# Laplacian filter: two adjacent image rows per partition instead of two half images, without pad columns

One core of a Trainium2 chip runs the kernel. The metric is the device time of one execution in microseconds, lower is better. The kernel before takes 40.27 us (median of 15 runs, 40.21 to 40.34).

## The reference

Input and output are float32 arrays of shape 8 x 3 x 256 x 256, that is 24 images of 256 KB each. Every image gets a five-point Laplacian whose missing neighbours at the border are the border pixels themselves.

```python
def reference(x):
    output = np.zeros_like(x)
    for b in range(batch):
        for ch in range(c):
            output[b, ch] = ndimage.laplace(x[b, ch])   # up + down + left + right - 4 * centre
    return output
```

6.29 MB are read and 6.29 MB are written. Nothing can be left out of either.

## The kernel before

Four images form a group of 1 MB; there are six groups. Partition `pp` holds row `pp` (half `h2 = 0`) and row `pp + 128` (half `h2 = 1`) of each image. The two rows are far apart in DRAM, so each contiguous run is one row: 1 KB. The tile has a pad column on either side of each row.

```python
raw = sbuf.tile([P, GROUP, 2, WP], fp32, name="raw", tag="raw")       # WP = W + 2
src = xi[g * GROUP:(g + 1) * GROUP].rearrange("img (h2 pp) w -> pp img h2 w", h2=2)
nc.sync.dma_start(out=raw[:, :, :, 1:W + 1], in_=src)                 # all six loads first
# ... then for each group:
nc.gpsimd.tensor_copy(out=raw[:, :, :, 0:1], in_=raw[:, :, :, 1:2])   # pads, on POOL
nc.gpsimd.tensor_copy(out=raw[:, :, :, WP - 1:WP], in_=raw[:, :, :, W:W + 1])
# ... three matmuls per 128x512 chunk (vertical terms, the other half's edge row, left neighbour)
nc.scalar.copy(out=oa, in_=pas[pr])                                   # PSUM to SBUF
nc.vector.tensor_add(out=oa, in0=oa, in1=r0)                          # right neighbour, float32
# ...
nc.scalar.dma_start(out=dst, in_=ot)                                  # store, issued by ACT
```

The matmuls read the upper two bytes of each float32 as bf16. Their weights (diagonals and single points) are built on POOL.

Of the kernel before, what the change touches and what calls it, by code (L numbers as in the profile page):

```python
# [1 line left out]

# [4 lines left out]


def _set_point(nc, mat_ap, p, f, val, n=128):  # L10
    cm = n + 1
    base = -(p * cm - f)
    nc.gpsimd.affine_select(  # L13
        out=mat_ap,
        in_=mat_ap,
        compare_op=mybir.AluOpType.not_equal,
        fill=float(val),
        base=base,
        pattern=[[-1, n]],
        channel_multiplier=cm,  # L20
    )


def _set_diagonal(nc, mat_ap, off, val, n=128):
    nc.gpsimd.affine_select(  # L25
        out=mat_ap,
        in_=mat_ap,
        compare_op=mybir.AluOpType.not_equal,
        fill=float(val),
        base=off,  # L30
        pattern=[[-1, n]],
        channel_multiplier=1,
    )


@with_exitstack
def kernel(
    ctx: ExitStack,
    tc: tile.TileContext,
    x: bass.AP,  # L40
    out: bass.AP,
):
    nc = tc.nc
    P = 128

    fp32 = mybir.dt.float32
    bf16 = mybir.dt.bfloat16

    B, C, H, W = x.shape
    assert H == 256 and W == 256  # L50
    NIMG = B * C
    xi = x.rearrange("b c h w -> (b c) h w")
    oi = out.rearrange("b c h w -> (b c) h w")

    GROUP = 4
    NG = NIMG // GROUP
    NPAIR = GROUP // 2
    WP = W + 2

    const_pool = ctx.enter_context(tc.tile_pool(name="consts", bufs=1))  # L60

    A = const_pool.tile([P, P], bf16, name="A_mat")
    Cm = const_pool.tile([P, P], bf16, name="C_mat")
    BT = const_pool.tile([P, P], bf16, name="BT_mat")
    Bm = const_pool.tile([P, P], bf16, name="B_mat")
    Ident = const_pool.tile([P, P], bf16, name="I_mat")

    nc.gpsimd.memset(A, 0.0)
    _set_diagonal(nc, A, 1, 1.0)
    _set_diagonal(nc, A, -1, 1.0)  # L70
    _set_diagonal(nc, A, 0, -4.0)
    _set_point(nc, A, 0, 0, -3.0)

    nc.gpsimd.memset(Cm, 0.0)
    _set_diagonal(nc, Cm, 1, 1.0)
    _set_diagonal(nc, Cm, -1, 1.0)
    _set_diagonal(nc, Cm, 0, -4.0)
    _set_point(nc, Cm, 127, 127, -3.0)

    nc.gpsimd.memset(BT, 0.0)  # L80
    _set_point(nc, BT, 0, 127, 1.0)

    nc.gpsimd.memset(Bm, 0.0)
    _set_point(nc, Bm, 127, 0, 1.0)

    nc.gpsimd.memset(Ident, 0.0)
    _set_diagonal(nc, Ident, 0, 1.0)

    sbuf = ctx.enter_context(tc.tile_pool(name="sbuf", bufs=6))
    psum = ctx.enter_context(tc.tile_pool(name="psum", bufs=4, space=bass.MemoryType.PSUM))  # L90

    raws = []
    for g in range(NG):
        raw = sbuf.tile([P, GROUP, 2, WP], fp32, name="raw", tag="raw")
        src = xi[g * GROUP:(g + 1) * GROUP].rearrange(
            "img (h2 pp) w -> pp img h2 w", h2=2
        )
        nc.sync.dma_start(out=raw[:, :, :, 1:W + 1], in_=src)
        raws.append(raw)

    for g in range(NG):
        raw = raws[g]
        nc.gpsimd.tensor_copy(out=raw[:, :, :, 0:1], in_=raw[:, :, :, 1:2])  # L103
        nc.gpsimd.tensor_copy(out=raw[:, :, :, WP - 1:WP], in_=raw[:, :, :, W:W + 1])  # L104

        rb = raw.bitcast(bf16)
        rb = rb.rearrange("pp img h (c two) -> pp img h c two", two=2)
        rb = rb[:, :, :, :, 1]

        ot = sbuf.tile([P, GROUP, 2, W], fp32, name="ot", tag="ot")  # L110

        pas = []
        pbs = []
        for pr in range(NPAIR):
            pas.append(psum.tile([P, 2, W], fp32, name="pa", tag="pa"))
            pbs.append(psum.tile([P, 2, W], fp32, name="pb", tag="pb"))

        def t0b(pr):
            i0 = 2 * pr
            return rb[:, i0:i0 + 2, 0, 1:W + 1]  # L120

        def t1b(pr):
            i0 = 2 * pr
            return rb[:, i0:i0 + 2, 1, 1:W + 1]

        def lshift_b(pr, h):
            i0 = 2 * pr
            return rb[:, i0:i0 + 2, h, 0:W]

        for pr in range(NPAIR):  # L130
            nc.tensor.matmul(pas[pr], A, t0b(pr), start=True, stop=False)  # L131
        for pr in range(NPAIR):
            nc.tensor.matmul(pbs[pr], Cm, t1b(pr), start=True, stop=False)  # L133
        for pr in range(NPAIR):
            nc.tensor.matmul(pas[pr], BT, t1b(pr), start=False, stop=False)  # L135
        for pr in range(NPAIR):
            nc.tensor.matmul(pbs[pr], Bm, t0b(pr), start=False, stop=False)  # L137
        for pr in range(NPAIR):
            nc.tensor.matmul(pas[pr], Ident, lshift_b(pr, 0), start=False, stop=True)  # L139
            nc.tensor.matmul(pbs[pr], Ident, lshift_b(pr, 1), start=False, stop=True)  # L140

        for pr in range(NPAIR):
            i0 = 2 * pr
            oa = ot[:, i0:i0 + 2, 0, :]
            ob = ot[:, i0:i0 + 2, 1, :]
            r0 = raw[:, i0:i0 + 2, 0, 2:WP]
            r1 = raw[:, i0:i0 + 2, 1, 2:WP]
            nc.scalar.copy(out=oa, in_=pas[pr])  # L148
            nc.vector.tensor_add(out=oa, in0=oa, in1=r0)  # L149
            nc.scalar.copy(out=ob, in_=pbs[pr])  # L150
            nc.vector.tensor_add(out=ob, in0=ob, in1=r1)  # L151

        dst = oi[g * GROUP:(g + 1) * GROUP].rearrange(
            "img (h2 pp) w -> pp img h2 w", h2=2
        )
        nc.scalar.dma_start(out=dst, in_=ot)  # L156


# [1 line left out]
_INS = ['x']  # L160
_OUTS = [((8, 3, 256, 256), 'float32')]


# [23 lines left out]
```

## Time and profile before

| | before |
|---|---|
| time, median | 40.27 us |
| span in the profile | 38.5 us |
| bytes moved, mean rate over the span | 12.58 MB, 327 GB/s |
| last store issued | 28.7 us |

The page of the profiled run, in this order: busy time of each engine; the busy share of the 16 DMA engines in 40 slices of the span; what they moved in each slice; the packet count; the shares of the chain of waits that ended last; and two groups of instructions (busy us and mean ns, then idle time before them).

```profile
PE 19.3 (50%) x72; PEld 7.3 (19%) x72; DVE 15.0 (39%) x24; ACT 13.7 (36%) x25; POOL 8.1 (21%) x32
...
DMA  0059989999999999999999999999999999999910
GB/s 0 6 176 381 387 275 318 379 362 352 347 349 347 351 348 349 348 346 349 356 387 387 387 383 386 388 383 387 388 383 387 387 386 386 386 385 387 334 46 0
DMA packets 12480, 12.58 MB, mean 327 GB/s; under 512 B 192, under 2 KB 12480, under 8 KB 12480
...
PE 23%; DMA 15%; ACT 11%; DVE 10%; issue 8%; POOL 2%; DVEq 2%; ACTq 1%; POOLq 0%
...
L103 POOL COPY raw<-raw 128x8 f32<-128x8 f32 x6 | 2.1, 358 | 15.3 <-DMA raw<-in_x_dram 15.3
...
L104 POOL COPY raw<-raw 128x8 f32<-128x8 f32 x6 | 2.6, 433 | 0.0
```

No compute engine is busy for much more than half of the span (PE 50%). The DMA row is at nine tenths almost throughout. All packets are under 2 KB; in the trace's single records, 12,288 of them are 1,024 bytes and 192 are the 4-byte completion marks. What the profile calls a packet is one contiguous run. The Trainium skill, "DMA: Bandwidth & Descriptors", section "Why a DMA increments its semaphore by 16 and not by 1", says that one descriptor moves one contiguous run, so the profile's packets are the skill's descriptors. The chain of waits names compute engines.

The view by stretches of time shows, per line, a stretch of the span, the busy time of each engine in it, the granted clock, the DMA share and, last, GB/s.

```profile
core 0: us, PE busy (x) PEld busy (x) DVE busy (x) ACT busy (x) POOL busy (x), PEclk, DMA share, GB/s
8.00:14.50 6.50, 6.43 (x21) 2.17 (x20) 2.50 (x4) 2.49 (x5) 1.46 (x5) 1.00 1.09 349
14.50:18.30 3.80, 3.80 (x18) 1.62 (x17) 3.31 (x6) 3.11 (x8) 1.18 (x2) 1.00 1.09 348
19.30:28.00 8.70, 6.56 (x28) 2.42 (x26) 7.49 (x13) 6.05 (x12) 0.85 (x3) 1.00 1.09 386
```

There are two rates: 348 to 349 GB/s while there are only loads, and 386 GB/s once stores run. In the single records a 1 KB packet takes 51 ns in the first case and 46 ns in the second.

The timeline of ACT shows the first and the last store being issued (start, duration, what).

```profile
14.53 0.41 ACTq L156 DMA_DIRECT2D out_dram<-ot  x1
...
28.72 0.69 ACTq L156 DMA_DIRECT2D out_dram<-ot  x1
```

The last store is issued at 28.72 us and the span ends at 38.5 us.

### The profile page before, as it was taken

To read this page: it belongs to the slowest core of one execution; us is meant where nothing else is said; L and a number is where in the kernel's file an instruction comes from. 1 tells how busy PE (TensorE), PEld (TensorE's weight loads), DVE (VectorE), ACT (ScalarE), POOL (GpSimd) and SP (SyncE) were. 2 spreads that over 40 slices of the span, in tenths; PEclk is the share of its full clock that TensorE was granted. 3 is DMA by queue.
4 is the path that set the end of the run, shared out by engine and by line. 5 is a ranking of instruction groups with operands and counts; after the bars stand their busy time and mean duration, and the time that the engine had idled before them with its cause. 6 is when DMAs were issued, how large, how long until landed. Compare 5 with 4: busy or idle time off the path is not lost.

```text
span 38.5 us, 302 instructions
## 1 busy us (share of the span) xinstructions
PE 19.3 (50%) x72; PEld 7.3 (19%) x72; DVE 15.0 (39%) x24; ACT 13.7 (36%) x25; POOL 8.1 (21%) x32
## 2 busy tenths in 40 slices
PE   0000002999999999999999989991000000000000
PEld 0001001332133444344434414330000000000000
DVE  0000000000019946998999996399870000000000
ACT  2900000000089339759795950993900000000000
POOL 4999102001400900830710007000000000000000
PEclk9999999999999999999999999999995555555555
DMA  0059989999999999999999999999999999999910
GB/s 0 6 176 381 387 275 318 379 362 352 347 349 347 351 348 349 348 346 349 356 387 387 387 383 386 388 383 387 388 383 387 387 386 386 386 385 387 334 46 0
DMA packets 12480, 12.58 MB, mean 327 GB/s; under 512 B 192, under 2 KB 12480, under 8 KB 12480
## 3 DMA queue, kind: packets, MB, share of 16 engines
q1 hardware_dynamic: 6240, 6.29, 49.8%
q10 hardware_dynamic: 6240, 6.29, 46.0%
HBM read 6.29 MB, written 6.29 MB: 327 GB/s over the span
## 4 chain that ended last, share of the span: by engine, by line
PE 23%; DMA 15%; ACT 11%; DVE 10%; issue 8%; POOL 2%; DVEq 2%; ACTq 1%; POOLq 0%
DMA raw<-in_x_dram 15%; ACT ot L148 9%; DVE ot L149 7%; PE pa L139 6%; PE pb L140 4%; DVE ot L151 4%; PE pa L135 4%; PE pa L131 4%; PE pb L133 3%; PE pb L137 3%; ACT ot L150 2%; DVEq L182 2%; ACTq L156 1%; POOL raw L103 1%; POOL raw L104 1%
## 5 line engine op out<-in xcount | busy, mean ns | idle before, releaser
L149 DVE TENSOR_TENSOR ot<-ot,raw 128x512 f32<-128x512 f32 x12 | 8.3, 688 | 13.7 <-ACT ot L148 12.6
L148 ACT COPY ot<-pa 128x512 f32<-128x512 f32 x12 | 7.1, 594 | 13.4 <-PE pa L139 10.9
L151 DVE TENSOR_TENSOR ot<-ot,raw 128x512 f32<-128x512 f32 x12 | 8.2, 682 | 0.0
L131 PE MATMUL pa<-raw,A_mat 128*128 128x512 bf16 x12 | 4.4, 427 | 6.7 <-DMA raw<-in_x_dram 6.7
L150 ACT COPY ot<-pb 128x512 f32<-128x512 f32 x12 | 7.2, 602 | 0.0
L103 POOL COPY raw<-raw 128x8 f32<-128x8 f32 x6 | 2.1, 358 | 15.3 <-DMA raw<-in_x_dram 15.3
L139 PE MATMUL pa<-raw,I_mat 128*128 128x512 bf16 x12 | 5.1, 426 | 0.1
L140 PE MATMUL pb<-raw,I_mat 128*128 128x512 bf16 x12 | 5.1, 425 | 0.0
L133 PE MATMUL pb<-raw,C_mat 128*128 128x512 bf16 x12 | 4.6, 431 | 0.0
L137 PE MATMUL pb<-raw,B_mat 128*128 128x512 bf16 x12 | 4.6, 429 | 0.0
L135 PE MATMUL pa<-raw,BT_mat 128*128 128x512 bf16 x12 | 4.5, 430 | 0.0
L131 PEld LDWEIGHTS <-A_mat 128*128 128x128 bf16 x12 | 1.2, 101 | 8.6 <-issue 4.0
L104 POOL COPY raw<-raw 128x8 f32<-128x8 f32 x6 | 2.6, 433 | 0.0
L139 PEld LDWEIGHTS <-I_mat 128*128 128x128 bf16 x12 | 1.2, 101 | 2.6 <-POOL I_mat L25 1.0
L135 PEld LDWEIGHTS <-BT_mat 128*128 128x128 bf16 x12 | 1.3, 105 | 1.9 <-issue 0.6
L137 PEld LDWEIGHTS <-B_mat 128*128 128x128 bf16 x12 | 1.3, 105 | 1.9 <-issue 0.6
L133 PEld LDWEIGHTS <-C_mat 128*128 128x128 bf16 x12 | 1.3, 105 | 1.8 <-issue 0.3
L148 ACT ACT_TABLE_LOAD x1 | 1.3, 1283 | 0.7 <-PEq L171 0.7
L140 PEld LDWEIGHTS <-I_mat 128*128 128x128 bf16 x12 | 1.2, 102 | 1.6 <-issue 0.3
L25 POOL TENSOR_SCALAR_AFFINE_SELECT A_mat<-A_mat 128x128 bf16<-128x128 bf16 x3 | 0.9, 296 | 0.0
L25 POOL TENSOR_SCALAR_AFFINE_SELECT C_mat<-C_mat 128x128 bf16<-128x128 bf16 x3 | 0.9, 296 | 0.0
L13 POOL TENSOR_SCALAR_AFFINE_SELECT BT_mat<-BT_mat 128x128 bf16<-128x128 bf16 x1 | 0.3, 298 | 0.0
(13 smaller groups left out, 2.6 us busy)
## 6 DMA issues: line engine op xcount, KB each, us to landing
raw<-in_x_dram SPq DMA_DIRECT2D x6, 1024.0 KB, 11.2
out_dram<-ot ACTq DMA_DIRECT2D x6, 1024.0 KB, 9.3
```

What stands on the lines that cost most here:

```text
L103: nc.gpsimd.tensor_copy(out=raw[:, :, :, 0:1], in_=raw[:, :, :, 1:2])
L104: nc.gpsimd.tensor_copy(out=raw[:, :, :, WP - 1:WP], in_=raw[:, :, :, W:W + 1])
L131: nc.tensor.matmul(pas[pr], A, t0b(pr), start=True, stop=False)
L133: nc.tensor.matmul(pbs[pr], Cm, t1b(pr), start=True, stop=False)
L135: nc.tensor.matmul(pas[pr], BT, t1b(pr), start=False, stop=False)
L137: nc.tensor.matmul(pbs[pr], Bm, t0b(pr), start=False, stop=False)
L139: nc.tensor.matmul(pas[pr], Ident, lshift_b(pr, 0), start=False, stop=True)
L140: nc.tensor.matmul(pbs[pr], Ident, lshift_b(pr, 1), start=False, stop=True)
L148: nc.scalar.copy(out=oa, in_=pas[pr])
L149: nc.vector.tensor_add(out=oa, in0=oa, in1=r0)
L150: nc.scalar.copy(out=ob, in_=pbs[pr])
L151: nc.vector.tensor_add(out=ob, in0=ob, in1=r1)
```

## The change

Each partition takes two *adjacent* rows, `2p` and `2p + 1`. Each run then is 2 KB on both sides. Because there are no pad columns, the border's left and right terms are added by POOL to the finished output, two columns at once. The matrices change with the rows: `U` and `L` each add the row above and the row below in one matmul, so the count of 72 matmuls stays.

```diff
-        raw = sbuf.tile([P, GROUP, 2, WP], fp32, name="raw", tag="raw")
+        raw = sbuf.tile([P, GROUP, 2, W], fp32, name="raw", tag="raw")
-            "img (h2 pp) w -> pp img h2 w", h2=2
+            "img (pp two) w -> pp img two w", two=2        # for the load and for the store
-        nc.sync.dma_start(out=raw[:, :, :, 1:W + 1], in_=src)
+        nc.sync.dma_start(out=raw, in_=src)
-        nc.gpsimd.tensor_copy(out=raw[:, :, :, 0:1], in_=raw[:, :, :, 1:2])
-        nc.gpsimd.tensor_copy(out=raw[:, :, :, WP - 1:WP], in_=raw[:, :, :, W:W + 1])
 ...
+                nc.tensor.matmul(pts[pr][s][:, :, 1:W], Ident, sub(pr, s)[:, :, 0:W - 1],
+                                 start=False, stop=True)
 ...
+                nc.vector.tensor_add(out=osl[:, :, 0:W - 1], in0=osl[:, :, 0:W - 1],
+                                     in1=raw[:, i0:i0 + 2, s, 1:W])
 ...
+        nc.gpsimd.tensor_add(out=ot[:, :, :, 0:W:W - 1], in0=ot[:, :, :, 0:W:W - 1],
+                             in1=raw[:, :, :, 0:W:W - 1])
```

More of the change, by code (lines that the diff above doesn't have):

```diff
@@ L56 @@
     NG = NIMG // GROUP
-    NPAIR = GROUP // 2
-    WP = W + 2
     const_pool = ctx.enter_context(tc.tile_pool(name="consts", bufs=1))
-    A = const_pool.tile([P, P], bf16, name="A_mat")
-    Cm = const_pool.tile([P, P], bf16, name="C_mat")
-    BT = const_pool.tile([P, P], bf16, name="BT_mat")
-    Bm = const_pool.tile([P, P], bf16, name="B_mat")
+    D0 = const_pool.tile([P, P], bf16, name="D0_mat")
+    D1 = const_pool.tile([P, P], bf16, name="D1_mat")
+    U = const_pool.tile([P, P], bf16, name="U_mat")
+    L = const_pool.tile([P, P], bf16, name="L_mat")
     Ident = const_pool.tile([P, P], bf16, name="I_mat")
-    nc.gpsimd.memset(A, 0.0)
-    _set_diagonal(nc, A, 1, 1.0)
-    _set_diagonal(nc, A, -1, 1.0)
-    _set_diagonal(nc, A, 0, -4.0)
-    _set_point(nc, A, 0, 0, -3.0)
-    nc.gpsimd.memset(Cm, 0.0)
-    _set_diagonal(nc, Cm, 1, 1.0)
-    _set_diagonal(nc, Cm, -1, 1.0)
-    _set_diagonal(nc, Cm, 0, -4.0)
-    _set_point(nc, Cm, 127, 127, -3.0)
-    nc.gpsimd.memset(BT, 0.0)
-    _set_point(nc, BT, 0, 127, 1.0)
-    nc.gpsimd.memset(Bm, 0.0)
-    _set_point(nc, Bm, 127, 0, 1.0)
+    nc.gpsimd.memset(D0, 0.0)
+    _set_diagonal(nc, D0, 0, -4.0)
+    _set_point(nc, D0, 0, 0, -3.0)
+    nc.gpsimd.memset(D1, 0.0)
+    _set_diagonal(nc, D1, 0, -4.0)
+    _set_point(nc, D1, 127, 127, -3.0)
+    nc.gpsimd.memset(U, 0.0)
+    _set_diagonal(nc, U, 0, 1.0)
+    _set_diagonal(nc, U, 1, 1.0)
+    nc.gpsimd.memset(L, 0.0)
+    _set_diagonal(nc, L, 0, 1.0)
+    _set_diagonal(nc, L, -1, 1.0)
     nc.gpsimd.memset(Ident, 0.0)
@@ L102 @@
         raw = raws[g]
-        nc.gpsimd.tensor_copy(out=raw[:, :, :, 0:1], in_=raw[:, :, :, 1:2])
-        nc.gpsimd.tensor_copy(out=raw[:, :, :, WP - 1:WP], in_=raw[:, :, :, W:W + 1])
         rb = raw.bitcast(bf16)
-        rb = rb.rearrange("pp img h (c two) -> pp img h c two", two=2)
+        rb = rb.rearrange("pp img two (c hi) -> pp img two c hi", hi=2)
         rb = rb[:, :, :, :, 1]
         ot = sbuf.tile([P, GROUP, 2, W], fp32, name="ot", tag="ot")
-        pas = []
-        pbs = []
@@ L114 @@
-        for pr in range(NPAIR):
-            pas.append(psum.tile([P, 2, W], fp32, name="pa", tag="pa"))
-            pbs.append(psum.tile([P, 2, W], fp32, name="pb", tag="pb"))
-        def t0b(pr):
-            i0 = 2 * pr
-            return rb[:, i0:i0 + 2, 0, 1:W + 1]
-        def t1b(pr):
-            i0 = 2 * pr
-            return rb[:, i0:i0 + 2, 1, 1:W + 1]
-        def lshift_b(pr, h):
-            i0 = 2 * pr
-            return rb[:, i0:i0 + 2, h, 0:W]
-        for pr in range(NPAIR):
-            nc.tensor.matmul(pas[pr], A, t0b(pr), start=True, stop=False)
@@ L132 @@
-        for pr in range(NPAIR):
-            nc.tensor.matmul(pbs[pr], Cm, t1b(pr), start=True, stop=False)
-        for pr in range(NPAIR):
-            nc.tensor.matmul(pas[pr], BT, t1b(pr), start=False, stop=False)
-        for pr in range(NPAIR):
-            nc.tensor.matmul(pbs[pr], Bm, t0b(pr), start=False, stop=False)
-        for pr in range(NPAIR):
-            nc.tensor.matmul(pas[pr], Ident, lshift_b(pr, 0), start=False, stop=True)
-            nc.tensor.matmul(pbs[pr], Ident, lshift_b(pr, 1), start=False, stop=True)
@@ L142 @@
-        for pr in range(NPAIR):
-            i0 = 2 * pr
-            oa = ot[:, i0:i0 + 2, 0, :]
-            ob = ot[:, i0:i0 + 2, 1, :]
-            r0 = raw[:, i0:i0 + 2, 0, 2:WP]
-            r1 = raw[:, i0:i0 + 2, 1, 2:WP]
-            nc.scalar.copy(out=oa, in_=pas[pr])
-            nc.vector.tensor_add(out=oa, in0=oa, in1=r0)
-            nc.scalar.copy(out=ob, in_=pbs[pr])
-            nc.vector.tensor_add(out=ob, in0=ob, in1=r1)
+        pts = [[psum.tile([P, 2, W], fp32, name=f"p{s}", tag=f"p{s}") for s in range(2)]
+               for _ in range(GROUP // 2)]
@@ new lines, with sub @@
+        prs = range(GROUP // 2)
+        def sub(pr, s):
+            return rb[:, 2 * pr:2 * pr + 2, s, :]
+        for pr in prs:
+            nc.tensor.matmul(pts[pr][0], D0, sub(pr, 0), start=True, stop=False)
+        for pr in prs:
+            nc.tensor.matmul(pts[pr][1], D1, sub(pr, 1), start=True, stop=False)
+        for pr in prs:
+            nc.tensor.matmul(pts[pr][0], U, sub(pr, 1), start=False, stop=False)
+        for pr in prs:
+            nc.tensor.matmul(pts[pr][1], L, sub(pr, 0), start=False, stop=False)
@@ new lines @@
+        for pr in prs:
+            for s in range(2):
+                nc.tensor.matmul(
+                    pts[pr][s][:, :, 1:W], Ident, sub(pr, s)[:, :, 0:W - 1],
+                    start=False, stop=True,
+                )
+        for pr in prs:
+            for s in range(2):
+                i0 = 2 * pr
+                osl = ot[:, i0:i0 + 2, s, :]
+                nc.scalar.copy(out=osl, in_=pts[pr][s])
+                nc.vector.tensor_add(
+                    out=osl[:, :, 0:W - 1],
+                    in0=osl[:, :, 0:W - 1],
+                    in1=raw[:, i0:i0 + 2, s, 1:W],
+                )
@@ L153 @@
+        nc.gpsimd.tensor_add(
+            out=ot[:, :, :, 0:W:W - 1],
+            in0=ot[:, :, :, 0:W:W - 1],
+            in1=raw[:, :, :, 0:W:W - 1],
+        )
         dst = oi[g * GROUP:(g + 1) * GROUP].rearrange(
-            "img (h2 pp) w -> pp img h2 w", h2=2
+            "img (pp two) w -> pp img two w", two=2
         )
```

## The prediction

> **What bounds it now.** Data movement. The per-slice DMA row is at nine tenths or more from about 3 to 37 us of the 38.5 us span, except for a dip around 5 to 6 us, while PE is busy 50%, DVE 39%, ACT 36%, POOL 21% (engine table). 12.58 MB move at 327 GB/s over the span. The timeline shows the last store issued at 28.7 us, yet stores still drain until about 37.5 us: compute has some 8 us of slack. The chain of waits names ACT, DVE and PE up to 28.7 us, but I read that as misleading; those pieces only fed a store queue that was already backed up.
>
> The DMA view cut into windows gives three regimes: loads alone from 8 to 18.3 us at 348 GB/s (median packet 51 ns), mixed loads and stores from 19.3 us and then stores alone up to 37 us at 386 to 387 GB/s (46 ns), and a start with a dip to 298 GB/s. All 12,288 data packets are 1 KB. At 387 GB/s one engine starts a packet every 42.3 ns.
>
> **What the change does.** Partition p holds rows 2p and 2p+1, and the two pad columns go, so each contiguous run is 2 KB on both sides: 6,144 data packets instead of 12,288, same bytes. PE keeps 72 matmuls (12 are almost as wide, 255 of 256 columns per row), ACT its 24 copies of 0.60 us, DVE its 24 adds of 0.685 us. The six pairs of POOL pad copies ahead of the matmuls (0.36 + 0.43 us each) become one 128x16 edge add per group after the DVE adds, ahead of the store; I estimate 0.3 to 0.7 us each from those copies. The identity matrix, which waited on POOL behind the second group's load (ready only at 10.1 us), gets ready near 4 us, so the first store issues perhaps 1 to 2 us earlier than 14.5 us. None of this compute is critical while the store queue is backed up.
>
> **Cost.** The Trainium skill, "DMA: Bandwidth & Descriptors", section "Why small descriptors are slow", gives a fixed cost of about 3 beats per packet next to 32 B beats. The 435 GB/s ceiling it states makes 37.6 ns for 1 KB; the trace's 42.3 ns leaves 4.7 ns (some 4 beats). Estimate: 2 KB every 80 ns, 410 GB/s.
> - Mixed and store stretch (6.9 MB, 18 us): 387 to about 407 GB/s, saves 0.85 us.
> - Load-only stretch (3.8 MB, 11 us): why it runs at 348 the trace doesn't tell. If half the gap to the store rate closes along with the packet cost, about 380 GB/s: saves 0.8 us; if it is a read limit indifferent to packet size, nothing. Fewer descriptors may also let stores join earlier, in the better regime.
> - Start and tail: about 0.1 us.
>
> Nearly all of this lies on the DMA path, so it shows in the time. Sum about 1.7 us.
>
> **Prediction: 38.6 us, 37.9 to 39.6.** Faster by over 2%: 0.82; within 2%: 0.16; slower: 0.02.
>
> **What would show it right.** Packets near 6,340; store-only GB/s at 400 to 412 with packets near 84 ns; load-only above 348; last store issued at 27 to 29.5 us with DMA still full until about 35.5 us; POOL edge adds below 1 us each and nobody waiting on them for long; first store issued at 12.5 to 14 us.
>
> **What would make it wrong.** Loads keep 348 GB/s (then about 39.4 us). The larger row pitch between partitions (2 KB) costs HBM reads. Stores join earlier and delay the last load so that the store queue runs dry before the last store is issued. The POOL add, held up by DVE, delays stores that ACT issues in order with its copies.

## The result

The changed kernel takes 38.2 us (median of 10 runs, 37.84 to 38.37) against 40.27 us. The ratio is 0.9467, 95% interval 0.944 to 0.9493. Such ratios are the mean time of one kernel's fast runs over that of the other's fast runs of the same rounds, so they are not quite the ratio of the medians quoted.

The same parts of the page of the changed kernel:

```profile
PE 19.1 (52%) x72; PEld 7.5 (21%) x72; DVE 14.9 (41%) x24; ACT 13.8 (38%) x25; POOL 5.9 (16%) x24
...
DMA  0049989999999999999999999999999999999710
GB/s 0 0 124 398 369 328 391 321 396 339 402 407 405 375 398 400 384 389 389 362 393 402 409 409 407 409 407 407 411 407 405 411 405 409 414 402 409 277 40 0
DMA packets 6336, 12.58 MB, mean 345 GB/s; under 512 B 192, under 2 KB 192, under 8 KB 6336
...
issue 52%; DMA 15%; POOL 7%; POOLq 1%
...
L139 POOL TENSOR_TENSOR ot<-ot,raw 128x16 f32<-128x16 f32 x6 | 2.6, 438 | 21.6 <-DVE ot L133 21.6
```

The packets have doubled in size and halved in number. PE, DVE and ACT are as busy as before, in us. The chain of waits has changed its face completely ("issue 52%") although only 2 us were won, which shows how little it said about the limit.

The same stretches of time:

```profile
core 0: us, PE busy (x) PEld busy (x) DVE busy (x) ACT busy (x) POOL busy (x), PEclk, DMA share, GB/s
8.00:14.50 6.50, 6.50 (x22) 2.41 (x21) 2.49 (x4) 2.56 (x6) 0.25 (x1) 1.00 1.03 389
14.50:18.30 3.80, 3.80 (x18) 1.60 (x17) 3.46 (x6) 3.04 (x7) 0.25 (x1) 1.00 1.05 382
19.30:28.00 8.70, 6.18 (x28) 2.41 (x26) 7.99 (x13) 5.92 (x12) 1.98 (x4) 1.00 1.05 408
```

Loads alone went from 349 to 389 and from 348 to 382 GB/s, the later stretch from 386 to 408 GB/s. In the single records a 2 KB packet takes 84 ns in stores and 84 to 88 ns in loads.

ACT's timeline around the first store, and its last store:

```profile
14.00 0.59 ACT L132 COPY ot<-p 128x512 f32<-128x512 f32 x1 [1.49 <-PE p L123]
14.46 0.42 ACTq L148 DMA_DIRECT2D out_dram<-ot  x1
...
28.18 0.38 ACTq L148 DMA_DIRECT2D out_dram<-ot  x1
```

The last store comes at 28.18 us, 0.5 us earlier than before, and the span ends 2.1 us earlier. The first store comes at 14.46 us, as good as unchanged. The list of who waited for whom (total us, times, longest) shows what the new POOL step costs ACT:

```profile
ACT ot L132 <- POOL ot L139: 1.9, 3, 0.9
```

It held ACT up three times, for at most 0.9 us. The stores were backed up, so this did not reach the time; the copy run below shows it.

**Where the 2 us came from.** By the single records, before moved 5.69 MB in 16.86 us until its first store packet, and the other 6.90 MB in 18.42 us. After moved 6.00 MB in 16.39 us and 6.59 MB in 16.89 us. At after's two rates, before's two parts would take 15.55 and 17.69 us. That is 1.3 us from the load part and 0.7 us from the rest. (Both are read from one profiled run of each kernel.)

### The profile page after: what moved, and what is told of

The parts are those of the page before. It is cut to its first block, busy times and chain, and to the rows that moved or that the text cites. A ratio compares the mean times of both kernels' runs of the same rounds, so it can differ in the third digit from the quotient of the medians.

```text
span 36.4 us, 297 instructions
## 1 busy us (share of the span) xinstructions
PE 19.1 (52%) x72; PEld 7.5 (21%) x72; DVE 14.9 (41%) x24; ACT 13.8 (38%) x25; POOL 5.9 (16%) x24
## 4 chain that ended last, share of the span: by engine, by line
issue 52%; DMA 15%; POOL 7%; POOLq 1%
DMA raw<-in_x_dram 15%; POOL ot L139 7%; POOLq L174 1%; POOLq L139 0%
## 5 line engine op out<-in xcount | busy, mean ns | idle before, releaser
L133 DVE TENSOR_TENSOR ot<-ot,raw 128x510 f32<-128x510 f32 x24 | 14.9, 689 | 12.9 <-ACT ot L132 12.9
L132 ACT COPY ot<-p 128x512 f32<-128x512 f32 x24 | 12.5, 597 | 12.6 <-PE p L123 10.6
L114 PE MATMUL p<-raw,D_mat 128*128 128x512 bf16 x12 | 4.7, 450 | 6.4 <-DMA raw<-in_x_dram 6.4
L123 PE MATMUL p<-raw,I_mat 128*128 128x510 bf16 x24 | 7.9, 427 | 0.0
L139 POOL TENSOR_TENSOR ot<-ot,raw 128x16 f32<-128x16 f32 x6 | 2.6, 438 | 21.6 <-DVE ot L133 21.6
L120 PE MATMUL p<-raw,L_mat 128*128 128x512 bf16 x12 | 4.6, 427 | 0.0
L116 PE MATMUL p<-raw,D_mat 128*128 128x512 bf16 x12 | 4.6, 427 | 0.0
L118 PE MATMUL p<-raw,U_mat 128*128 128x512 bf16 x12 | 4.4, 427 | 0.0
L114 PEld LDWEIGHTS <-D_mat 128*128 128x128 bf16 x12 | 1.3, 105 | 7.9 <-issue 4.9
L116 PEld LDWEIGHTS <-D_mat 128*128 128x128 bf16 x12 | 1.3, 108 | 2.0 <-issue 1.0
L120 PEld LDWEIGHTS <-L_mat 128*128 128x128 bf16 x12 | 1.2, 104 | 1.9 <-issue 0.6
L118 PEld LDWEIGHTS <-U_mat 128*128 128x128 bf16 x12 | 1.2, 103 | 1.9 <-issue 0.6
```

The source lines that it names most:

```text
L114: nc.tensor.matmul(pts[pr][0], D0, sub(pr, 0), start=True, stop=False)
L116: nc.tensor.matmul(pts[pr][1], D1, sub(pr, 1), start=True, stop=False)
L118: nc.tensor.matmul(pts[pr][0], U, sub(pr, 1), start=False, stop=False)
L120: nc.tensor.matmul(pts[pr][1], L, sub(pr, 0), start=False, stop=False)
L123: nc.tensor.matmul(pts[pr][s][:, :, 1:W], Ident, sub(pr, s)[:, :, 0:W - 1], start=False, stop=True,)
L132: nc.scalar.copy(out=osl, in_=pts[pr][s])
```

## The experiments

Theory A: the size of the packets is the cause, for loads and stores alike, and the compute side adds nothing. Theory B: the compute side (pad copies gone, identity matrix ready early). Theory C: the loads were slow because of the pad, which shifted their targets by 4 bytes, or because of the row order.

### Old rows, new compute

```diff
-            "img (pp two) w -> pp img two w", two=2
+            "img (two pp) w -> pp img two w", two=2        # load and store; matrices to match
```

> The old row mapping (1 KB packets both ways) with the new compute: no pad columns, no pad copies, edge add on POOL. Theory A (the packet size is the cause): no gain, 40.0 to 40.4 us, stores alone at 386 GB/s, loads alone at 348. Theory B (the compute side: pad copies gone, identity ready early): 38.2 us. Theory C (loads were slowed by the pad, which made their targets start 4 bytes off): loads alone near 387 GB/s, stores at 386, about 39.2 us.

Measured: 40.32 us, ratio 0.9971 (0.9928 to 1.0013). From its page:

```profile
PE 18.2 (47%) x72; PEld 7.2 (19%) x72; DVE 15.0 (39%) x24; ACT 13.8 (36%) x25; POOL 6.0 (16%) x26
...
GB/s 0 14 136 303 389 328 322 303 380 375 351 346 351 349 348 348 349 349 348 389 385 384 389 383 385 389 386 383 388 386 384 388 386 384 388 388 385 373 56 0
DMA packets 12480, 12.58 MB, mean 327 GB/s; under 512 B 192, under 2 KB 12480, under 8 KB 12480
```

1 KB packets and the slow rates are back (346 to 351 GB/s for loads, then 383 to 389), although the pads and the pad copies are gone and each target starts on a row boundary of the tile. Theory B falls, and so does the pad part of theory C.

### Cutting the transfers in two, four ways

Cutting a load or store by row parity leaves the new layout and compute alone and makes its packets 1 KB. Cutting it by images keeps 2 KB and is the control for the doubled count of transfers.

```diff
-        nc.sync.dma_start(out=raw, in_=src)
+        for s in range(2):                                  # 1 KB; the same for the store
+            nc.sync.dma_start(out=raw[:, :, s, :], in_=src[:, :, s, :])
+        for i in (0, 2):                                    # control: 2 KB
+            nc.sync.dma_start(out=raw[:, i:i + 2], in_=src[:, i:i + 2])
```

Both cut to 1 KB:

> Both cuts: 12,288 packets of 1 KB with the new rows and the new compute. Theory A: the whole gain is lost, 40.0 to 40.5 us, loads alone 348, stores alone 386. Theories B and C: 38.2 to 39.2 us.

Measured: 40.51 us, ratio 1.0041 (0.9974 to 1.0109). The whole gain is lost with the new rows in place, so the row order alone is not the cause either. The GB/s row of its page has 347 to 351 while there are only loads and 381 to 389 in stores, as before the change.

Control, both cut, 2 KB:

> Control for the cut transfers: the changed kernel with every load and store cut in two by images, so 24 transfers of 512 KB but still 2 KB packets. Theory A: the cutting itself costs nothing, 38.0 to 38.5 us. If cutting costs, then part of what the runs with 1 KB packets lost was due to it: 38.6 us or more.

Measured: 38.31 us (37.88 to 38.61), ratio 0.9392 (0.9351 to 0.9432). Two of its four runs were marked slow (over 1.5% above its fastest) and are left out of the ratio. The median of all four lies within the range of the changed kernel's runs (37.84 to 38.37 us). So cutting in itself costs nothing that shows.

Only stores cut to 1 KB:

> The changed kernel with each store cut in two by row parity: loads 2 KB, stores 1 KB. Theory A: loads as in the changed kernel (372 GB/s on average over the load), stores alone back at 386 GB/s, about 39.1 us. Theory B: 38.2 us.

Measured: 38.91 us, ratio 0.9645 (0.9581 to 0.971). Its stretches of time:

```profile
10.50:14.50 4.00, 4.00 (x17) 1.62 (x16) 2.68 (x5) 2.87 (x6) 0.25 (x1) 1.00 1.05 395
14.50:18.30 3.80, 3.80 (x19) 1.60 (x17) 3.58 (x6) 2.35 (x6) 0.25 (x1) 1.00 1.05 386
22.00:34.00 12.00, 3.17 (x15) 1.15 (x12) 5.80 (x10) 4.69 (x9) 1.50 (x3) 0.77 1.09 385
```

Loads run at 386 to 395 GB/s and stores at 385. Against the changed kernel's ratio the loss is 0.018 of 40.3 us, or 0.7 us, give or take 0.3 us by the two intervals: that is the worth of the larger store packets.

Only loads cut to 1 KB:

> The changed kernel with each load cut in two by row parity, so that loads move in 1 KB packets and stores in 2 KB. Theory A: stores alone 408 GB/s, loads back at 348 to 355 in the load-only stretch, about 39.2 us. Theory B: 38.2 us. Theory C (row order or alignment, not size, sped the loads): loads stay near 387, about 38.3 us.

Measured: 39.92, 40.56, 41.65 and 44.17 us. Three of the four are over 1.5% above the fastest, so there is no ratio, and this run does not settle what it was made for. Its profile, which is of the slow run of 41.65 us, shows something else. It was the only run of this kernel that was profiled, so it is not known whether the others have the same. First the DMA rows of its page:

```profile
DMA  0079999999999999999999999999994009999940
GB/s 0 1 256 375 372 246 343 320 367 380 358 347 353 347 347 350 361 400 398 402 396 405 402 399 404 400 401 408 406 413 173 0 19 387 387 366 389 376 183 0
```

There is a hole of some 2 us near the end. The queues in the stretch from 18.5 to 24.5 us (q10 is the stores', q1 the loads': packets, MB, share):

```profile
q10 hardware_dynamic: 808, 1.59, 68.3%
q1 hardware_dynamic: 814, 0.81, 38.0%
```

Both queues got the same *number* of packets, 808 and 814, so the 2 KB stores got twice the bytes of the 1 KB loads. The Trainium skill, "DMA: Bandwidth & Descriptors", section "Queues, rings and completion order", says that each DMA engine goes round robin between its queues, a packet at a time. A packet in the skill's sense holds several descriptors; equal counts agree with turns of equally many descriptors on both queues, whatever their size. The loads were starved (by the single records the last load packet ended 26.1 us after the first began, against 19.0 us in the changed kernel), and the compute ran out of input (two lines of ACT's timeline, then one of PE's):

```profile
24.51 0.58 ACT L133 COPY ot<-p 128x512 f32<-128x512 f32 x1 [0.69 <-PE p L124]
30.97 1.07 ACT L133 COPY ot<-p 128x512 f32<-128x512 f32 x2 [5.87 <-PE p L124]
...
28.46 0.40 PE L117 MATMUL p<-raw,D_mat 128*128 128x512 bf16 x1 [3.29 <-DMA raw<-in_x_dram]
```

PE waited 3.29 us for a load and ACT 5.87 us for PE; then PE ran slowly (granted clock 0.50 from 29.5 to 31.5 us, matmuls 0.43 us apart instead of 0.23). The store queue ran dry before the last stores were ready: no packet began for 2.1 us. The run with both sides cut, which has 1 KB packets on both of the same two queues, has no such hole. So I put this down to unequal packets on two queues that share the engines, not to the 1 KB packets themselves. How much of the time of the four runs it explains was not measured.

### Loads of 1 KB without the starvation

Both runs issue the stores from SP, behind the loads on one queue, so that stores cannot overtake loads. The second also cuts the loads to 1 KB.

```diff
-        nc.scalar.dma_start(out=dst, in_=ot)
+        nc.sync.dma_start(out=dst, in_=ot)
```

> The changed kernel with the stores issued from SP, behind the loads on the same queue, so that no store competes with a load. Theory A: the data path stays full, so 38.0 to 38.4 us as the changed kernel; loads alone 372 to 380 GB/s on average, stores alone 408. It is the base for the next run. If stores joining late or early mattered to the total, it would differ from 38.2 by more than 0.4 us.

> As the run before, but loads cut into 1 KB packets. It repeats the earlier run with 1 KB loads without the starvation seen there (2 KB store packets took two thirds of the engines while both queues had work, the last load came late and the store queue ran dry). Theory A: loads 330 to 348 GB/s, stores 408, the whole load takes 1.0 to 1.6 us longer than in the run before and the total is 0.9 to 1.5 us longer, near 39.4 us. If load packet size did not matter once starvation is gone: equal to the run before.

Measured: 38.12 us with 2 KB loads (ratio 0.9448, 0.9398 to 0.9498) and 39.5 us with 1 KB loads (ratio 0.9767, 0.9717 to 0.9817, one run of four marked slow and left out). By the 2% rule the verdict on the second against the kernel before is unclear. Here it is compared with the first, which ran in the same rounds: the fast means are 38.10 and 39.38 us, 1.3 us apart, while the fast runs of either kernel spread over 0.3 to 0.5 us. Stretches of time with 2 KB loads:

```profile
10.50:14.50 4.00, 4.00 (x20) 1.69 (x18) 3.32 (x6) 3.27 (x8) 0.24 (x1) 1.00 1.05 400
14.50:18.30 3.80, 3.80 (x19) 1.58 (x18) 3.58 (x7) 2.66 (x6) 0.24 (x1) 1.00 1.05 388
22.00:34.00 12.00, 2.53 (x12) 0.86 (x9) 4.78 (x8) 3.29 (x7) 0.49 (x2) 0.72 1.05 408
```

and with 1 KB loads (this profile fell on the run marked slow, so only its rates are read, and they equal those of before):

```profile
10.50:14.50 4.00, 4.00 (x18) 1.68 (x17) 2.84 (x5) 2.40 (x6) 0.25 (x1) 1.00 1.10 348
14.50:18.30 3.80, 3.80 (x19) 1.59 (x18) 3.58 (x7) 2.49 (x6) 0.25 (x1) 1.00 1.10 349
22.00:34.00 12.00, 2.59 (x12) 0.86 (x9) 4.75 (x8) 3.26 (x7) 0.49 (x2) 0.75 1.05 409
```

Loads at 388 to 400 against 348 to 349 GB/s, stores at 408 and 409. So the load packets are worth 1.3 us and the store packets 0.7 us, each within some 0.3 us; together that is the 2.0 us of the change, and it agrees with the sum from the single records above. The first of the two runs also shows that it makes no difference to the total whether stores mix with loads or follow them.

### Data movement alone, with 2, 4 and 8 KB

These three compute nothing: each group is stored as it was loaded, from SP. Their outputs are wrong, which doesn't matter for the times.

```diff
+    def rows(t, g):                       # R = 4 or 8 rows per partition; 2 KB keeps the changed rows
+        v = t[g * GROUP:(g + 1) * GROUP].rearrange("img h w -> (img h) w")
+        return v.rearrange("(b q r) w -> q b (r w)", q=P, r=R)
 ...
+        nc.sync.dma_start(out=rows(oi, g), in_=raws[g])
```

> Wrong on purpose: no compute, the changed kernel's 2 KB mapping, stores behind loads on SP's queue. It tells where the slower start of the loads (330 to 390 GB/s in the first 7 us) comes from, which the copy runs with 4 and 8 KB don't show. If from the packet size or the address pattern: the slow start is there, about 38.0 us. If from the compute side's own traffic or timing: loads near 405 GB/s from the start and about 37.4 us.

> Wrong on purpose: no compute, each group is loaded and stored unchanged, with runs of 4 KB (four rows per partition), all on SP's queue. Theory A, with a packet costing 4.1 ns plus 38.2 ns per KB (from 42.3 ns at 1 KB and 80.4 ns at 2 KB): stores alone at 417 GB/s, one packet every 157 ns, about 37.3 us. If the rate levels off at 2 KB: 408 GB/s and about 37.9 us.

> As the run before with runs of 8 KB (eight rows per partition). Theory A: stores alone at 423 GB/s, about 37.0 us. If packets are cut at 4 KB: as the run with 4 KB, 6,144 / 2 packets of 4 KB.

Measured: 38.01 us (2 KB), 36.66 us (4 KB), 36.62 us (8 KB).

**2 KB.** The ratio is 0.9408 (0.9355 to 0.9462), against 0.9448 (0.9398 to 0.9498) for the full kernel with stores from SP. The changed kernel runs at the speed of its data movement; its compute is hidden. The Trainium skill, "SBUF — State Buffer", section "SBUF: two separate sides", says that DMA and engine accesses to SBUF do not slow each other; this agrees. From its page:

```profile
POOL 0.2 (1%) x4
...
GB/s 0 2 137 315 392 385 398 394 349 311 351 392 396 394 407 405 389 389 387 380 389 416 405 405 421 401 405 419 401 405 419 403 407 414 405 407 412 279 41 0
```

The slow stretch early in the loads (349, 311, 351 GB/s) is there without any compute. It is absent with 4 KB:

```profile
GB/s 0 0 80 390 423 399 432 418 418 427 413 418 404 418 404 413 409 409 409 296 315 451 404 423 427 399 451 404 423 427 399 451 404 423 427 399 451 348 24 0
```

and with 8 KB, whose packets were not cut (1,536 of 8,192 bytes in the single records):

```profile
GB/s 0 0 151 386 414 405 443 443 424 433 424 396 452 433 424 433 424 396 283 245 235 424 443 414 405 414 443 452 433 414 405 414 443 452 433 433 396 330 75 0
```

So the slow start belongs to the transfers, either to their packet size or to their addresses; these runs do not tell which. Its absence is probably why the 4 KB run beat its estimate of 37.3 us. Both larger sizes dip where loads hand over to stores (296 and 315, and 235 to 283 GB/s). The cause is open; with 8 KB it ate the gain over 4 KB.

**The cost of a packet.** A 1 MB store finishes every 2.717 us with 1 KB packets (before), 2.566 us with 2 KB, 2.491 us with 4 KB and 2.453 us with 8 KB, by the completion marks. Divided by the 64, 32, 16 and 8 packets that each of 16 engines moves for it, one packet takes 42.5, 80.2, 155.7 and 306.6 ns. These four lie within 0.3 ns of 4.7 ns + 37.7 ns per KB. The prediction had 80 ns for 2 KB from the 1 KB figure and the 435 GB/s ceiling that the Trainium skill states in the specifications of "DMA: Bandwidth & Descriptors"; the runs confirm both terms.

### A candidate with 4 KB packets and correct results

Four rows per partition give 4 KB packets, but a row's two vertical neighbours no longer share a tile row, so PE needs four matmuls per chunk, 96 in all. Twelve dummy matmuls run during the first load, to have PE at its short matmul time early: its matmuls are 0.23 us apart from 7.1 us on, where in the kernel before they are 0.43 us apart until 11.8 us. Stores go from SP.

```diff
+        for s in range(R):                                  # R = 4
+            up = (U, R - 1) if s == 0 else (Ident, s - 1)
+            dn = (L, 0) if s == R - 1 else (Ident, s + 1)
+            nc.tensor.matmul(p, diag, rb[:, :, s, :], start=True, stop=False)
+            nc.tensor.matmul(p, up[0], rb[:, :, up[1], :], start=False, stop=False)
+            nc.tensor.matmul(p, dn[0], rb[:, :, dn[1], :], start=False, stop=False)
+            nc.tensor.matmul(p[:, :, 1:W], Ident, rb[:, :, s, 0:W - 1], start=False, stop=True)
```

> A candidate with correct results: four rows per partition (4 KB packets), stores on SP's queue, twelve dummy matmuls to have PE at its short matmul time when the first load lands; PE needs 96 matmuls instead of 72. Estimate: PE 96 x 0.229 us = 22 us from 6.4 us, done near 28.4 us, last store issued near 30 us; the data path alone (copy run with 4 KB) would need it by about 29.7 us. Theory A: 36.9 to 37.4 us, against 36.66 us for the copy run and 38.2 us for the changed kernel. If PE becomes the limit: a hole in the DMA row before the last store, 37.5 us or more.

Measured: 37.78 us, correct, ratio 0.9355 (0.9323 to 0.9386). That is better than the changed kernel, but 1.1 us above the copy run. From its page:

```profile
PE 27.2 (76%) x108; PEld 11.0 (31%) x108; DVE 16.8 (47%) x25; ACT 15.3 (43%) x25; POOL 5.6 (16%) x28
...
GB/s 0 0 101 394 408 412 431 435 408 412 431 403 412 417 403 412 403 408 385 275 408 426 426 417 417 421 431 398 408 426 426 417 417 412 224 417 394 247 9 0
```

PE is busy 76% of the span, and the GB/s row has a hole (224) near the end: the last store, issued at 30.15 us, came too late to keep the queue full. That looked like the limit, so one matmul in sixteen went to DVE:

```diff
-            nc.tensor.matmul(p, dn[0], rb[:, :, dn[1], :], start=False, stop=False)
+            if s != 1:
+                nc.tensor.matmul(p, dn[0], rb[:, :, dn[1], :], start=False, stop=False)
 ...
+            if s == 1:
+                nc.vector.tensor_add(out=of[:, :, s, :], in0=of[:, :, s, :], in1=rf[:, :, s + 1, :])
```

> The 4 KB candidate with one of its 16 matmuls per group taken from PE and done as one more full-width DVE add (0.605 us apart back to back, and DVE was 47% busy). The candidate's trace showed PE as the limit: last store issued at 30.15 us and a hole in the DMA row before it of some 0.7 us. Estimate: six matmuls of 0.226 us fewer, last store issued near 28.8 us, hole gone, 36.8 to 37.1 us against 37.78. If the hole was not PE's doing, no change: 37.7 us.

Measured: 37.74 us, correct, ratio 0.9324 (0.9293 to 0.9355). The hole closed and the last store came at 28.3 us, yet the time hardly moved. That expectation failed. Its page:

```profile
GB/s 0 0 105 362 421 421 421 417 426 421 421 403 417 394 426 398 417 412 389 307 417 435 403 430 417 435 394 417 417 421 417 421 426 421 417 421 362 27 9 0
...
q1 hardware_dynamic: 3264, 12.58, 87.4%
q8 instruction: 1, 0.02, 0.2%
```

and the last 3 us of its DMA activity in 40 slices of 0.075 us:

```profile
DMA  9999691401010101010101010000000000000000
GB/s 382 492 382 437 273 492 55 164 0 55 0 55 0 55 0 55 0 55 0 55 0 55 0 55 0 0 0 0 0 0 0 0 0 0 0 0 0 0 0 0
```

The tail at 55 GB/s in every other slice is one 4 KB packet per two slices: a single DMA engine at work, long after the others. In the single records, 15 of the 16 engines mark the last store as done by 31.34 us after the first load packet and the last one at 32.55 us. The first candidate ends in the same way: 15 engines by 31.91 us, the last at 32.55 us. So in both profiles one late engine set the time. In the first it worked on without a pause while the others stood in the hole, so closing the hole could not help; that is why the expectation failed. The line of q8 is a fetch of instructions: one packet of 16 KB that took 931 ns, 21.3 us after the first load packet (21.7 us in the first candidate). Both candidates have it; neither the changed kernel nor the copy runs have one once their loads have begun. The completion marks fit it closely. In the second candidate the marks of the store before the fetch lie within 0.42 us of each other. In the store that it falls into, one mark comes 0.8 us after the latest of the others, and in every later store 1.2 us after. A 4 KB packet that starts as the fetch ends takes 435 ns instead of 159; with the 931 ns that makes 1.2 us. In the first candidate one engine is 0.85 us behind the others from the first store after the fetch on, until the others stand in the hole, and the packet at the end of the fetch takes 441 ns. So I take it that this engine lost its time there. The two traces agree on that, but no run removed the fetch, so it is not shown by experiment. A shorter program, or one without the 24 warm-up instructions, is the next thing to try.

Both candidates beat both kernels: their intervals lie below that of the changed kernel. The step from 0.9467 to 0.9324 is about 1.5%, less than the 2% at which a verdict counts, and the runs are of different rounds.

## Why the prediction was right, point by point

- **DMA bounds it, and the compute has slack.** Right. The copy run with 2 KB takes 38.01 us and the full kernel 38.12 us. New compute on old rows gave nothing (40.32 us). Only the size of the slack, "some 8 us", was too large: the last store must also be moved, which leaves about 5 us (the estimate above).
- **The chain of waits is misleading here.** Right. What it named (ACT, DVE, PE) did not change in busy time, and the time fell by 2 us.
- **A packet of 2 KB every 80 ns, stores near 410 GB/s.** Right: 80.2 ns and 408 GB/s. The estimate was 0.85 us; the run with cut stores gives 0.7 us.
- **Loads: half of the gap to the store rate, 0.8 us.** Right in direction, but in part luck. The prediction said that it did not know why loads ran at 348 GB/s, and "half" was a guess between all and nothing. Loads alone ran at 382 to 389 GB/s, close to its 380, and the pair with stores from SP puts the term at 1.3 us. The term was also too small because it counted only 3.8 MB of loads, on which these rates save about 1.0 us (an estimate); the rest came from the first 8 us. This is why 38.2 us came out instead of 38.6. Part of what the loads gained lies in a stretch late in the loads in which each packet takes some 4 to 5 ns more than in stores (51 against 46 ns at 1 KB, 88 against 84 at 2 KB, 164 against 159 at 4 KB, in the single records). A fixed extra per packet shrinks with fewer packets. At 8 KB it was not seen. It is not confined to loads: the last store of the first 4 KB candidate, issued into an empty queue, has 164 ns too. What causes it is open.
- **First store 1 to 2 us earlier.** Wrong, and without consequence: 14.46 against 14.53 us. The identity matrix was indeed ready early, but PE had other matmuls to do until about then, so its identity matmuls began only 0.34 us earlier (9.79 against 10.13 us). And ACT issues the store in order, behind copies of the second group that wait for PE.
- **Stores may join the loads earlier.** They did not, to speak of: the first store packet came 16.4 us after the first load packet, against 16.9. About 4 us passed between issue and first packet in both kernels; the runs do not explain it. By the run with stores from SP it does not matter.
- **POOL's edge add stays off the critical path.** Right: 0.25 to 0.63 us each, and ACT waited for it three times, 1.9 us in all, while stores were backed up.

## What to carry to other kernels

When the DMA row is full from end to end, count the packets before counting instructions: here a packet cost 4.7 ns beside its bytes, a layout with neighbouring rows in one partition bought bandwidth, and the change of compute alone bought nothing. Check what binds by running the data movement alone; when the full kernel equals it, stop tuning compute. A hole in the DMA row shared by most engines need not set the time: look at which engine ends last. And try equal packet sizes on queues that run at the same time: in the one profile here with unequal ones, each queue got the same count of packets, and the loads, whose packets were half as large, starved.

## What the Trainium skill lacked or had wrong

- "DMA: Bandwidth & Descriptors", section "Why small descriptors are slow", counts about 3 cycles per packet in its example. The runs show 4.7 ns beside 37.7 ns per KB, which is 4.0 beats of 32 bytes. The section also names 32 bytes of descriptor metadata per operation; they would make the fourth beat (an estimate from the page; no run separates the two), but the example leaves them out.
- The same page's specifications table says that 512 B and more reach line rate. Stores reached 386 GB/s at 1 KB, 409 at 2 KB, 421 at 4 KB and 427 at 8 KB (1 MB over the times between completion marks), so the step from 1 to 4 KB is worth 9%.
- The same page, section "Where 436 GB/s comes from", says that some 358 GB/s of HBM bind transfers between HBM and SBUF. One core here stored at 408 GB/s and loaded at 382 to 389. (The same section goes on to call a measured 425 GB/s near the fabric rate, and "HBM Reference", section "Specifications (TRN2)", says that a core alone exceeds its share, so the pages do not agree in this.)
- The same page does not draw the consequence of its round robin: with 2 KB stores beside 1 KB loads, 808 and 814 packets moved in 6 us, the loads got half the bytes; later in that run the store queue stood empty for 2.1 us.
- No page that I found mentions the extra 4 to 5 ns per packet late in a series of loads (51 against 46 ns at 1 KB), nor the dip where loads hand over to stores (to 235 GB/s at 8 KB).
- "Runtime: NRT & Kernel Launch", section "Instruction fetch mechanics", says that instructions are refilled in 16 KiB blocks over a DMA queue and that the cost is mostly hidden. It does not say that such a block occupies one of the engines that move the data: one 16 KB packet took 931 ns, and one engine was 1.2 us late from then on (two candidates show this; no run removed the fetch).
